# Gates behind the attention, recurrence and readouts ranked ahead, meta queries two blocks earlier, output projections in held order: a two-layer hybrid decoder trunk on one core

## The chip, the core and the metric

The kernel runs on one core of a Trainium2 chip. A core has TensorE (PE; its weight loads are listed as PEld), VectorE (DVE), ScalarE (ACT), GpSimd (POOL) and SyncE (SP), which here only issues DMAs. The metric is the device time of one execution in microseconds.

## The reference

The trunk has two layers of width 1024 over 16 learned meta tokens and 1024 tokens. One projection feeds two mixers: sliding-window attention with sinks (16 heads of 64, 2 key-value heads, meta tokens always visible) and an mLSTM matrix memory in chunkwise form (4 heads). Both are gated, concatenated and projected back.

```python
def hybrid_layer(x, ...):
    z = rms_norm(x, norm_g) @ w_in
    aq, ak, av, ag, mq, mk, mv, mi, mf, mo, mgate = split(z)
    q, k = rope(rms_norm(aq)), rope(rms_norm(ak))
    ya = sliding_window_sink_attention(q, k, av, sink) * silu(ag)
    mq, mk = split(silu(causal_conv(concat(mq, mk), conv_w, conv_b)))
    log_i, log_f = mi + b_i, log_sigmoid(mf + b_f)
    hm = rms_norm(mlstm_chunkwise(mq, mk, mv, log_i, log_f))
    ym = hm * sigmoid(mo) * silu(mgate)
    return x + concat(ya, ym) @ w_out
```

All of it is float32; the output is the 1024 token rows after the second layer.

## The kernel before

**Precision.** A float32 product is made of three fast ones: each operand is split into a rounded part (hi, an ACT copy) and the rest (lo, a subtraction on DVE or POOL), and hi*hi, hi*lo and lo*hi are summed in PSUM. So each weight tile and each activation needs a split before PE can use it. The tile `H` holds the normalised input of a layer, hi in rows 0 to 7 and lo in 8 to 15; in the output projection its 16 rows hold the hi parts of the 16 gated mixer outputs (`y`), and the units `ylo` hold their lo parts.

**Tiles.** The 1040 rows are cut into one tile of 16 (the meta tokens) and eight of 128 (`TT`), and for transposed results into three chunks of 272, 384 and 384 columns (`CH`).

**Memory that rotates.** `units` (16 large buffers), `t384` (5), `p512` (4), `w1k` (5), `raw` (2 buffers for weights as they land) and `RING` (8 split weight pairs) are pools: who takes a buffer waits until its last user is done. PSUM has eight banks: `pj` (2) for projections throughout, and either `S`, `T`, `O` for the attention or `pt`, `pss`, `po` (2 each) for the rest.

**Order.** A scheduler takes instructions in the order in which the program writes them, lets a ready one pass one that is not, and fixes an order for each engine before the run; each engine then works through its own queue in that order. `tc.high_priority(offset=EARLY)` ranks what stands in it 80 places ahead; `pin` keeps PE's instructions in the written order while `in_order` is set, which is the case from the first query projections to the end of the attention (L1000 on) and nowhere in the output projection.

**A layer.**
- `kv_tasks`: keys and values of all nine tiles, projected by `projN` from `H`.
- Attention: eight pairs of heads `j`, each of nine query blocks (eight in layer 1, where the meta block isn't needed). A block goes through `s1` (scores, mask, exponential, scale), `s2` (transposes of the probabilities and their split, L665 to L679), `s3` and `s4` (products with the values, readout at L707, gate), each some steps behind the other, woven with the query, gate and value projections of the next pairs (L222). In layer 0 the meta queries of pair j + 1 are transposed in `s3` of block 5 of pair j, in the bank of its result, and split into their unit by `q_put` (L561 to L564) in `s4` of the same block. The first block of pair j + 1 then uses them.
- `gates`: the log gates and their running sums and maxima for the whole sequence (L732 to L775), a serial chain over ACT, DVE and PE, written after the attention.
- mLSTM: for each of the four heads nine chunks in three steps `sa`, `sb`, `sc_` (state update, numerator and denominator, transposed result), woven with the remaining projections: values (`v_tasks`), convolution (`conv_tasks`) and output gates (`mo_tasks`). Their PSUM results are read out by an ACT instruction each (L793, L819, L838, L841).
- Output projection: all 16 `y` are loaded from DRAM (`spool`) and split first (L1100 to L1109, 48 splits in all), then four groups follow: the tiles up to 4 with the left and the right half of the columns, then tiles 5 to 8 with the left and the right half. A group runs 16 weight tiles (`wout`: load L172, hi on ACT L174, lo L175 on DVE for every third, else on POOL) against its tiles, 3 products of 512 columns each (L1135). The last group keeps its last 8 weights and finishes tile by tile. For a finished tile the residual is loaded (L1154), added (L1157) and stored; in layer 0 the sum of squares is taken (L1162) and, with the right half, `norm_tile` normalises the tile and transposes it into `H` (L277 to L292) for the next layer.

Of the kernel before, what the change touches and what calls it, by code (L numbers as in the profile page):

```python
# [62 lines left out]
def build(ctx, tc, I, O):  # L63
# [103 lines left out]

    def wout(l, k, c0, i):
# [3 lines left out]
        sy.dma_start(raw, I["w_out"][l][k * 128:(k + 1) * 128, c0:c0 + 512])  # L172
        hi, lo = [pair[:, a].rearrange("p a b -> p (a b)")[:, 0:512] for a in range(2)]
        sc.activation(hi, raw, AF.Copy)  # L174
        (ve if i % 3 == 2 else gp).tensor_tensor(lo, raw, hi, op=ALU.subtract)  # L175
# [98 lines left out]
    def norm_tile(t, xh, ssq_ap, gbc):  # L274
# [5 lines left out]
        for g in range(2):  # L280
            if gbc is None:
                ve.tensor_scalar(xh[g][:p, :], xh[g][:p, :], v[:p, 1:2], None, ALU.mult)
            for i in range(2 if gbc is not None else 0):
                xs = xh[g][:p, 256 * i:256 * i + 256]
                ve.scalar_tensor_tensor(xs, xs, v[:p, 1:2], gbc[2 * g + i][:p, 0:256], ALU.mult, ALU.mult)
            ps = bank("pt")
            for k in range(4):
                pin(pe.transpose(ps[:, k * p:(k + 1) * p], xh[g][:p, k * 128:(k + 1) * 128], ident[:p, :p]))
            src = ps[:, 0:4 * p].rearrange("p (k t) -> p k t", k=4)
            hi = H[:, 4 * g:4 * g + 4, t0:t0 + p]  # L290
            sc.activation(hi, src, AF.Copy)
            ve.tensor_tensor(H[:, 8 + 4 * g:12 + 4 * g, t0:t0 + p], src, hi, op=ALU.subtract)  # L292
            if t == 0:
                for i in range(3):
                    ve.tensor_copy(HM[:, 4 * g:4 * g + 4, 16 * i:16 * i + 16],
                                   H[:, 4 * (g + i // 2 * 2):4 * (g + i // 2 * 2) + 4, 0:16])
# [15 lines left out]
    def first_norm(t, xt, G):  # L312
# [9 lines left out]
        norm_tile(t, xg, st[:p, 0:2], None)  # L322
# [29 lines left out]

    for l in range(DEPTH):
# [11 lines left out]
        SS = []  # L365
        blk = [0, 0]
# [85 lines left out]
        def kv_tasks():  # L452
# [161 lines left out]
        def att_tasks(j, st):  # L614
# [67 lines left out]
            def s3(b):  # L682
# [12 lines left out]
            def s4(b):  # L695
# [10 lines left out]
                with tc.high_priority(offset=EARLY):  # L706
                    sc.activation(up[0:64, 0:2 * p], O[64:128, 0:2 * p], AF.Copy)  # L707
# [19 lines left out]
        def gates(GR):  # L727
# [4 lines left out]
            sc.activation(e, zf, AF.Abs)  # L732
# [54 lines left out]
        def v_tasks(h, wgf, st):  # L787
            def tile_task(t):
                p = TT[t][1]
                if t == 0:  # L790
                    v_units(st)
                ps = projN(wgf(), t, 256)
                sc.activation(st["V"](t)[:p, 0:256], ps[:p, 0:256], AF.Copy)  # L793
# [14 lines left out]
        def conv_tasks(h, wgf, st):  # L808
            def chunk_task(which, c):
# [9 lines left out]
                sc.activation(RAW[:, 3 + t0:3 + t0 + n], ps[:, :n], AF.Copy)  # L819
# [10 lines left out]
        def mo_tasks(u, wgf, st, held=None):  # L830
            def chunk_task(c):
# [6 lines left out]
                sc.activation(t1, ps[:, :n], AF.Tanh, scale=0.5)  # L838
                ps = projT(wgf(), 128, a, n)
                t2 = t384(n)  # L840
                sc.activation(t2, ps[:, :n], AF.Tanh, scale=0.5)  # L841
                ve.scalar_tensor_tensor(t2, t2, 1.0, ps[:, :n], ALU.add, ALU.mult)
# [11 lines left out]
        def m_tasks(h, st):  # L854
# [12 lines left out]
            def mm_split(out, a, b):  # L867
                for i, (x, y) in enumerate(((a[0], b[0]), (a[0], b[1]), (a[1], b[0]))):
                    pin(pe.matmul(out, x, y, start=(i == 0), stop=(i == 2)))

            def sa(c):
# [11 lines left out]
                if c < 8:  # L883
                    pk = bank("pt")
                    pin(pe.transpose(pk[:p, 0:128], kc, ident))
# [19 lines left out]
                pin(pe.matmul(pS[:p, :p], kc, qc, start=True, stop=True))  # L905
# [42 lines left out]
            def sc_(c):  # L948
# [5 lines left out]
                for f in range(2):  # L954
                    pin(pe.transpose(ph[:, 128 * f:128 * f + p], hs[:p, 128 * f:128 * f + 128], ident[:p, :p]))
# [4 lines left out]

            out = [begin]
            for c in range(11):
                if c < 9:
                    out.append(lambda c=c: sa(c))
                if 0 <= c - 1 < 9:
                    out.append(lambda c=c - 1: sb(c))
                if 0 <= c - 2 < 9:
                    out.append(lambda c=c - 2: sc_(c))
# [125 lines left out]
        for i, k in enumerate(order):  # L1094
# [92 lines left out]
```

## Time and profile before

| | us |
|---|---|
| median of 3 runs | 1997.38 |
| lowest and highest run | 1996.06, 1997.59 |
| the profiled execution | 1995.97 |
| its span (first to last instruction) | 1994.2 |

| busy in the span | PE | PEld | DVE | ACT | POOL |
|---|---|---|---|---|---|
| us | 1916.2 | 1806.1 | 1099.9 | 1062.6 | 929.9 |

The stages lie, by the timeline, at about 0 to 86 us (first norm, keys, first queries), 86 to 428 (attention), 428 to 828 (gates and mLSTM) and 828 to 1045 (output projection and norm) in layer 0, and up to 1394, 1800 and 1991 for the same ends in layer 1. A row of a window gives its length, each engine's busy time with the count of instructions, the granted share of PE's clock, the DMA share and GB/s. A row of a timeline gives start, length, engine, line, operation, output and inputs, count, and in brackets the idle time before it with what ended it. Matmuls overlap in PE, so one of 512 columns is listed with some 400 ns though one starts every 232 ns.

### The profile page before, as it was taken

What the parts mean: (1) busy time and instruction counts of PE and PEld (TensorE: products, weight loads), DVE (VectorE), ACT (ScalarE), POOL (GpSimd) and SP (SyncE); (2) the same over time, 40 slices, a digit from 0 to 9 for tenths busy, and PEclk for the clock granted to TensorE, in tenths of its full rate; (3) what the DMA queues carried; (4) which work ended last, traced back from release to release, by engine and by line L of the source; (5) the groups of instructions that cost most, each with busy time, mean ns of one, the idle gap of its engine ahead of it and who ended that gap; (6) DMA issues with size and microseconds to landing.
All of it is one profiled execution on the core that took longest, in us unless ns stands there. A gap on an engine that the chain in (4) does not pass through costs nothing. (4 is left out here: it accounts for less than half of the span.)

```text
span 1994.2 us, 36168 instructions
## 1 busy us (share of the span) xinstructions
PE 1916.2 (96%) x12823; PEld 1806.1 (91%) x12823; DVE 1099.9 (55%) x2969; ACT 1062.6 (53%) x3133; POOL 929.9 (47%) x1116
## 2 busy tenths in 40 slices
PE   6999899999999999989999999999999999999899
PEld 6899899999999999867879999999999999997787
DVE  8767767666445364541435677776573636347111
ACT  5567767655454544642324678777364545446221
POOL 7544544335555454553335345444365453646331
PEclk9999999999999999999999999999999999999999
DMA  5111111111212122453541111112122221217443
GB/s 160 43 33 42 42 44 37 35 53 45 57 47 69 36 59 58 146 170 115 162 144 49 48 36 51 45 36 58 38 58 62 39 76 38 61 47 232 145 141 106
DMA packets 149796, 147.71 MB, mean 74 GB/s; under 512 B 14952, under 2 KB 122768, under 8 KB 149616
## 3 DMA queue, kind: packets, MB, share of 16 engines
q1 hardware_dynamic: 149616, 145.41, 25.1%
q8 instruction: 101, 1.65, 0.4%
q14 instruction: 79, 0.65, 0.1%
HBM read 122.01 MB, written 23.29 MB: 73 GB/s over the span
## 5 line engine op out<-in xcount | busy, mean ns | idle before, releaser
L183 PE MATMUL pj<-H,RING 128*128 128x384 f32 (+2 forms) x3456 | 578.4, 323 | 0.3 <-ACT t L838 0.3
L183 PEld LDWEIGHTS pj<-H,RING 128*128 128x128 f32 x3456 | 546.1, 189 | 2.9 <-issue 0.7
L160 POOL TENSOR_TENSOR RING<-raw,RING 128x512 fp32r<-128x512 f32 (+1 forms) x196 | 260.6, 1337 | 137.8 <-ACT RING L159 125.4
L222 PE MATMUL pj<-RING,H 128*128 128x256 f32 (+1 forms) x1920 | 270.0, 287 | 1.9 <-DVE w1k L190 1.9
L222 PEld LDWEIGHTS pj<-RING,H 128*128 128x128 f32 x1920 | 244.0, 190 | 2.3 <-DVE w1k L190 2.2
L222 PE MATMUL pj<-H,RING 128*128 128x384 f32 (+2 forms) x1152 | 217.7, 327 | 3.0 <-DVE u L564 3.0
L175 POOL TENSOR_TENSOR RING<-raw,RING 128x512 fp32r<-128x512 f32 x88 | 115.0, 1311 | 196.8 <-ACT RING L174 192.4
L183 PE MATMUL pj<-RING,H 128*128 128x256 f32 x1536 | 200.8, 285 | 2.6 <-DVE H L292 1.5
L183 PEld LDWEIGHTS pj<-RING,H 128*128 128x128 f32 x1536 | 189.0, 189 | 4.0 <-DVE H L292 1.7
L174 ACT ACTIVATE RING<-raw 128x512 fp32r<-128x512 f32 x128 | 80.7, 632 | 202.2 <-DMA raw<-in_w_out_dram 134.1
L222 PEld LDWEIGHTS pj<-H,RING 128*128 128x128 f32 x1152 | 180.7, 191 | 3.8 <-PE T L668 1.3
L159 ACT ACTIVATE RING<-raw 128x512 fp32r<-128x512 f32 (+1 forms) x196 | 122.9, 629 | 73.3 <-DMA raw<-in_w_in_dram 48.2
L713 POOL TENSOR_TENSOR u<-u,w1k 128x128 f32<-128x128 f32 (+1 forms) x136 | 63.4, 466 | 176.8 <-DVE w1k L709 169.4
L175 DVE TENSOR_TENSOR RING<-raw,RING 128x512 fp32r<-128x512 f32 x40 | 31.5, 788 | 194.0 <-ACT RING L174 194.0
L679 POOL TENSOR_SCALAR_AFFINE_SELECT p<-p 128x512 fp32r<-128x512 f32 x112 | 72.2, 645 | 133.7 <-DVE p L675 131.1
L649 ACT ACTIVATE t<-S,mx 128x145 f32<-128x145 f32 (+1 forms) x272 | 100.3, 373 | 62.6 <-DVE mx L646 54.5
L882 POOL TENSOR_TENSOR p<-u,p 128x258 fp32r<-128x258 f32 x64 | 46.7, 730 | 169.2 <-ACT p L881 169.1
L1135 PE MATMUL pj<-RING,H 128*128 128x512 f32 x352 | 112.9, 400 | 7.1 <-DVE p L1157 5.8
L1135 PE MATMUL pss<-RING,H 128*128 128x512 f32 x352 | 113.5, 402 | 1.3 <-ACT H L1104 1.3
L824 DVE SCALAR_TENSOR_TENSOR t<-u,cw,t 128x384 f32<-128x384 f32 (+1 forms) x144 | 109.1, 757 | 2.6
L628 PE MATMUL S<-u 128*128 128x272 f32 (+2 forms) x544 | 87.5, 280 | 19.3 <-DVE u L563 16.3
L654 ACT ACTIVATE t<-t,mx 128x144 f32<-128x144 f32 (+1 forms) x272 | 97.6, 406 | 13.6 <-DVE mx L651 13.1
(342 smaller groups left out, 3834.0 us busy)
## 6 DMA issues: line engine op xcount, KB each, us to landing
raw<-in_w_out_dram SPq DMA_DIRECT2D x128, 256.0 KB, 2.8
raw<-in_w_in_dram SPq DMA_DIRECT2D x100, 256.0 KB, 2.8
raw<-in_w_in_dram SPq DMA_DIRECT2D x192, 128.0 KB, 2.3
spool<-u SPq DMA_DIRECT2D x56, 192.0 KB, 1.9
p<-x SPq DMA_DIRECT2D x24, 256.0 KB, 4.4
t<-spool SPq DMA_DIRECT2D x28, 192.0 KB, 3.5
p<-spool SPq DMA_DIRECT2D x28, 192.0 KB, 3.6
u<-em SPq DMA_DIRECT2D x8, 576.0 KB, 6.9
```

Of the source, the lines that this page charges most:

```text
L159: sc.activation(hi, raw[:, :, 0:o], AF.Copy)
L160: eng.tensor_tensor(lo, raw[:, :, 0:o], hi, op=ALU.subtract)
L174: sc.activation(hi, raw, AF.Copy)
L175: (ve if i % 3 == 2 else gp).tensor_tensor(lo, raw, hi, op=ALU.subtract)
L183: pin(pe.matmul(out, a, b, start=(i == 0), stop=(i == n - 1)))
L222: pin(pe.matmul(out(), x, y, start=(k + i == 0), stop=(k == n - 1 and i == 2)))
L628: pin(pe.matmul(S[:p, h, o + 2 - 2 * h:o + 2 - 2 * h + kn], lq, Ks[i][:, k0:k0 + kn], start=(i == 0), stop=(i == 1)))
L649: sc.activation(P[:p, 145 * h:145 * h + 145], S[:p, h, 1 + 127 * h:146 + 127 * h], AF.Exp, bias=mx[:p, 0, h:h + 1], accum_out=mx[:p, 1, h: ...
L654: sc.activation(Pn, Pn, AF.Copy, scale=mx[:p, 2, h:h + 1])
L679: gp.affine_select(OW, HL, [[0, 4], [1, 128]], ALU.is_ge, 0.0, base=0, channel_multiplier=-1)
L824: ve.scalar_tensor_tensor(z, RAW[:, t0 + i:t0 + i + n], wcol(i), z, ALU.mult, ALU.add)
L1135: pin(pe.matmul(ps[:p, :], a, b, start=(i + n == 0), stop=(i == 15 and n == len(terms) - 1)))
```

## The change

It has five parts. None adds or removes a product.

1. **Meta queries**: they are transposed and split in block 3 instead of block 5 of the pair before.
2. **Gates**: the first gate instruction on ACT is placed behind the attention's last readout (L707) by `tc.issue_after`.
3. **Ranks**: the readouts of the value, convolution and output-gate projections are ranked 80 places up. So are all steps of the recurrence (`ranked`), except its PE instructions (`there`), which keep their rank.
4. **Output projection**: the groups after the first keep the written order on PE. The splits of `y` are written between the weights: chunks 0 and 1 in the first group, chunk 2 in the second. Banks go in pairs. Three weights (six in the last group) are kept for the tile-by-tile end. Residual loads are issued behind the last weight load before them. The lo part of a weight goes to DVE for i = 9, 11, 13, 15 only.
5. **Norm between the layers**: `norm_tile` is cut into `norm_pre` (scale) and `norm_half` (four transposes and the split). Tiles 0 to 4 are reloaded and normalised during the third group, tiles 5 to 8 in the last; what is left over (`carry`) is run between the key projections of layer 1.

```diff
     def wout(l, k, c0, i):
-        sy.dma_start(raw, I["w_out"][l][k * 128:(k + 1) * 128, c0:c0 + 512])
+        w_load[0] = sy.dma_start(raw, I["w_out"][l][k * 128:(k + 1) * 128, c0:c0 + 512]).ins
...
-        (ve if i % 3 == 2 else gp).tensor_tensor(lo, raw, hi, op=ALU.subtract)
+        (ve if i > 8 and i % 2 else gp).tensor_tensor(lo, raw, hi, op=ALU.subtract)
...
                 ps = projN(wg, t, 256)
+                if l > 0 and t != 1 and carry:
+                    carry.pop(0)()
...
-                if b == 5 and j < 7 and first_q == 0:
+                if b == 3 and j < 7 and first_q == 0:
...
-                    sc.activation(up[0:64, 0:2 * p], O[64:128, 0:2 * p], AF.Copy)
+                    att_end[0] = sc.activation(up[0:64, 0:2 * p], O[64:128, 0:2 * p], AF.Copy).ins
...
-            sc.activation(e, zf, AF.Abs)
+            with tc.issue_after(att_end[0]):
+                sc.activation(e, zf, AF.Abs)
...
-                sc.activation(RAW[:, 3 + t0:3 + t0 + n], ps[:, :n], AF.Copy)
+                with tc.high_priority(offset=EARLY):
+                    sc.activation(RAW[:, 3 + t0:3 + t0 + n], ps[:, :n], AF.Copy)
...
+            def there(f, *a, **k):
+                with tc.high_priority(offset=-EARLY):
+                    pin(f(*a, **k))
...
-                    out.append(lambda c=c: sa(c))
+                    out.append(lambda c=c: ranked(sa, c))
...
-        pools = ["pj", "pss", "po"]
+        pools = ["pj", "pj", "pss", "pss", "po", "po"]
...
+            with tc.issue_after(w_load[0]):
+                sy.dma_start(xr[:p, :], src)
...
+        def norm_again(t):
+            t0, p = TT[t]
+            x = [p512(F32) for _ in range(2)]
+            for i in range(2):
+                sy.dma_start(x[i][:p, :], x1[t0:t0 + p, 512 * i:512 * i + 512])
+            norm_later(t, [y[:, o:o + 256] for y in x for o in (0, 256)])
...
+            in_order[0] = g > 0
...
+            cut = 10 if g == 3 else 13
+            chunks = ((0, 1), (2,), (), ())[g]
+            for i in range(cut):
+                for c in chunks:
+                    y_split(i, c)
+                w = wout(l, order[i], c0, i)
                 for t in grp:
+                    product(pss_t[t], i, t, w)
+                if g == 2 and not last:
+                    if i > 2:
+                        turn()
+                    if i % 2 and i < 10:
+                        norm_again(i // 2)
...
+            for t in grp:
+                for i, w in tail:
+                    product(pss_t[t], i, t, w)
+                    if g == 3 and i == 12:
+                        turn(3)
+                if g == 3:
+                    turn(2)
+                result(pss_t[t], t, hf)
+        in_order[0] = False
+        carry[:] = turns
```

`turn` runs the oldest waiting `norm_half` if enough of them wait; `norm_later` runs `norm_pre` and queues the two halves.

More of the change, by code (lines that the diff above doesn't have):

```diff
@@ L321, in first_norm @@
             xg.append(y)
-        norm_tile(t, xg, st[:p, 0:2], None)
+        norm_pre(t, xg, st[:p, 0:2], None)
+        for g in range(2):
+            norm_half(t, g, xg[g:g + 1])
     snk = cp.tile([128, 2, HEADS], F32, name="snk")
@@ L365, in build @@
         SS = []
+        att_end = [None]
         blk = [0, 0]
@@ L868, in mm_split @@
                 for i, (x, y) in enumerate(((a[0], b[0]), (a[0], b[1]), (a[1], b[0]))):
-                    pin(pe.matmul(out, x, y, start=(i == 0), stop=(i == 2)))
+                    there(pe.matmul, out, x, y, start=(i == 0), stop=(i == 2))
+            def there(f, *a, **k):
+                with tc.high_priority(offset=-EARLY):
+                    pin(f(*a, **k))
             def sa(c):
@@ L884, in sa @@
                     pk = bank("pt")
-                    pin(pe.transpose(pk[:p, 0:128], kc, ident))
+                    there(pe.transpose, pk[:p, 0:128], kc, ident)
                     kt = KQ[:p, 0:128], KQ[:p, 128:256]
@@ L959, in sc_, with ranked @@
                                   scale=cw[:, l, 40 + u:41 + u])
+            def ranked(f, c):
+                with tc.high_priority(offset=EARLY):
+                    f(c)
             out = [begin]
@@ new lines, in build, with product @@
+        pools = ["pj", "pj", "pss", "pss", "po", "po"]
+        nb = [0]
+        turns = []
+        def product(ps, i, t, w):
+            k = order[i]
+            t0, p = TT[t]
+            wh, wl = w
+            if t == 0:
+                st = ylo[k][:, L:L + 48]
+                terms = ((st, wh), (st, wl))
+                p = 48
+            else:
+                hi, lo = H[:, k, t0:t0 + p], ylo[k][:, t0:t0 + p]
+                terms = ((hi, wh), (hi, wl), (lo, wh))
+            for n, (a, b) in enumerate(terms):
+                pin(pe.matmul(ps[:p, :], a, b, start=(i + n == 0), stop=(i == 15 and n == len(terms) - 1)))
@@ new lines, in result @@
+        def result(ps, t, hf):
+            t0, p = TT[t]
+            c0 = 512 * hf
+            xr = p512(F32)
+            if l > 0:
+                src = x1[t0:t0 + p, c0:c0 + 512]
+            elif t == 0:
+                src = I["meta"][:, c0:c0 + 512]
+            else:
+                src = I["x"][t0 - 16:t0 + 112, c0:c0 + 512]
+            with tc.issue_after(w_load[0]):
+                sy.dma_start(xr[:p, :], src)
+            if t == 0:
+                ve.tensor_tensor(xr[:16, :], ps[32:48, :], xr[:16, :], op=ALU.add)
+            ve.tensor_tensor(xr[:p, :], ps[:p, :], xr[:p, :], op=ALU.add)
+            if last:
+                sy.dma_start(O["out"][t0 - 16:t0 + 112, c0:c0 + 512], xr[:p, :])
+                return
+            if hf == 1 and t > 4:
+                x0 = [t384(256) for _ in range(2)]
+                for i, x in enumerate(x0):
+                    sy.dma_start(x[:p, :], x1[t0:t0 + p, 256 * i:256 * i + 256])
+            sy.dma_start(x1[t0:t0 + p, c0:c0 + 512], xr[:p, :])
+            sc.activation(bank("pt")[:p, :], xr[:p, :], AF.Square, accum_out=ssq[:p, t, hf:hf + 1])
+            if hf == 1 and t > 4:
+                norm_later(t, x0 + [xr[:, 0:256], xr[:, 256:512]])
```

157 lines of the change are left out of this document (66 added, 91 removed).

## The prediction

> **What bounds the kernel now.** I read the page first, then a table of busy time by stage, then the list of TensorE's own waits, and then the timeline at the longest of them. The page says which engine carries the span:
>
> ```profile
> span 1994.2 us, 36168 instructions
> PE 1916.2 (96%) x12823; PEld 1806.1 (91%) x12823; DVE 1099.9 (55%) x2969; ACT 1062.6 (53%) x3133; POOL 929.9 (47%) x1116
> ```
>
> TensorE is busy for 96%, and the change adds and removes no matmul. So the change can win only what PE idles (1994.2 - 1916.2 = 78 us), and what PE loses to a lower clock after an idle stretch. By stage (columns: length, then busy PE, weight loads, VectorE, ScalarE, GpSimd, granted clock):
>
> ```profile
> 450.00:800.00 350.00, 347.73 (x2423) 341.75 (x2422) 175.32 (x515) 177.16 (x532) 183.52 (x236) 1.00 0.20 53
> 1450.00:1750.00 300.00, 300.00 (x2102) 297.31 (x2102) 152.59 (x431) 150.14 (x440) 158.90 (x198) 1.00 0.23 57
> ```
>
> The mLSTM stage, where the ranks change, is full (350 - 347.7 = 2.3 us idle in layer 0, none in layer 1): ranking can win nothing there. The idle time lies elsewhere, and PE's wait list names it (total us, times, longest):
>
> ```profile
> PE S L628 <- DVE u L563: 16.3, 8, 5.9
> ...
> PE T L665 <- DVE ptm L676: 6.3, 4, 2.8
> PE pj L1135 <- DVE p L1157: 5.8, 1, 5.8
> ...
> PE pj L1135 <- POOL RING L175: 2.3, 1, 2.3
> PE po L869 <- DVE w1k L933: 2.1, 2, 1.1
> ...
> PE po L1135 <- ACT RING L174: 1.8, 1, 1.8
> ...
> PE pj L1135 <- ACT H L1104: 1.3, 1, 1.3
> PE po L1135 <- POOL RING L175: 1.3, 2, 0.7
> PE pss L1135 <- ACT H L1104: 1.3, 1, 1.3
> ```
>
> Three parts of the change meet three of these groups: the meta queries (L563, 16.3), the end of the attention (L676, 6.3) and the output projection (L1135: 5.8 + 2.3 + 1.8 + 1.3 + 1.3 + 1.3 = 13.8). Short windows around the gaps show the clock, the figure after the busy times:
>
> ```profile
> 248.00:254.00 6.00, 5.65 (x37) 5.51 (x38) 3.29 (x12) 2.76 (x11) 4.27 (x4) 0.70 0.33 90
> 328.00:334.00 6.00, 4.18 (x23) 4.04 (x24) 3.51 (x12) 2.90 (x11) 5.04 (x4) 0.72 0.39 105
> 414.00:420.00 6.00, 4.71 (x20) 4.74 (x21) 4.46 (x11) 2.48 (x5) 2.42 (x5) 0.72 0.24 63
> ...
> 894.00:900.00 6.00, 6.00 (x22) 4.73 (x22) 0.78 (x3) 2.18 (x7) 1.28 (x1) 0.77 0.83 253
> ...
> 1394.00:1400.00 6.00, 6.00 (x29) 6.00 (x28) 3.01 (x8) 2.25 (x4) 1.47 (x4) 0.72 0.17 44
> ...
> 1856.00:1863.00 7.00, 5.44 (x13) 4.37 (x14) 3.08 (x5) 1.86 (x4) 2.55 (x2) 0.52 0.65 210
> ```
>
> A busy stretch of 6 us at 0.72 loses 0.28 x 6 = 1.7 us. So a removed gap also returns about 1.7 us of clock.
>
> **The change part by part.**
>
> *Meta queries two blocks up.* In layer 0 each pair's first block (16 queries) waits for the split of its meta queries, which is now transposed in block 3 instead of 5, so some two blocks earlier:
>
> ```profile
> L628 PE MATMUL S<-u 128*16 128x16 f32 x32 | 3.1, 174 | 16.0 <-DVE u L563 15.4
> ```
> ```profile
> 241.45 0.92 PE L222 MATMUL pj<-H,RING 128*128 128x272 f32 x6
> 248.27 0.50 PE L628 MATMUL S<-u 128*16 128x16 f32 x4 [5.90 <-DVE u L563]
> ```
> ```profile
> 244.94 0.71 ACT L654 ACTIVATE t<-t,mx 128x144 f32<-128x144 f32 x2
> ```
>
> The whole wait is 15.4 us. What is late next is the softmax scale of the block before (L654), without which PE's next transposes (L665) can't run. In the longest case 13 matmuls stand before them, no more than 2 us by the row of 6 in 0.92: PE would come to them between 244.0 and 244.4. But the scale ends at 244.94 + 0.71 = 245.65: I let 1.7 us stay. For the six short gaps together I take 1.2 us that stay (an estimate: most are no longer than the work that stands between). Gain 15.4 - 2.9 = 12.5 us; bounds 7 and 15.4. Of the clock I count the loss at 328 alone, 1.7 us; the one at 248 may stay with its remainder. **14.2 us.** The instructions that move (a 16-column transpose, two small ACT copies, two small DVE subtractions) are the same and move on PE, ACT and DVE alone; their unit of memory is taken two blocks earlier, when the first half of the old queries has just been read for the last time.
>
> *Gates behind the attention.* The gates' Abs, Exp and Ln stand in ScalarE's queue ahead of the attention's last copies, with a table load:
>
> ```profile
> 410.95 1.28 ACT L734 ACT_TABLE_LOAD   x1
> ...
> 427.76 0.38 ACT L707 ACTIVATE w1k<-O 64x256 f32<-64x256 f32 x1 [0.83 <-PE O L704]
> ```
> ```profile
> 415.29 0.27 PE L665 MATMUL T<-cst,t 128*32 128x128 f32 x1 [2.85 <-DVE ptm L676]
> ...
> 432.21 0.27 PE L737 MATMUL po<-cst,GT 128*36 128x128 f32 x1
> ```
> ```profile
> 1393.77 0.27 PE L665 MATMUL T<-cst,t 128*32 128x128 f32 x1 [2.43 <-DVE ptm L676]
> ```
>
> The copies L672 and L673 come late by it, and PE's next transposes wait 2.85 us here and 2.43 in layer 1: 5.3 us. I leave 0.5 in each for the copy's own chain: 4.3, and 2 x 1.7 of clock (rows 414 and 1394). **7.7 us.** The added wait: the Abs now stands behind the last L707, which ends at 428.1. With the 1.28 load and some 0.9 of small work the gates end near 430.4, before PE takes their transposes at 432.2; so it costs nothing, and behind the waiting Abs stand the convolution's copies, which two banks of projection cover. If that cover fails, the recurrence begins up to 2 us later in each layer: bounds of this cost -4 to +5.3.
>
> *Readouts and recurrence 80 places up.* They reorder ACT, DVE and POOL in a stage in which PE is full, while the recurrence's matmuls keep their rank. Value 0; from the trace at most the 2.3 us idle above to win, and on the other side the third rival.
>
> *Output projection.* The splits of the gated outputs spread (32 in the first group, 16 in the second, instead of all 48 ahead); the groups after the first keep the written order on PE; banks rotate in pairs; VectorE takes no weight split before the tenth. The longest gap shows what this meets:
>
> ```profile
> 1856.21 0.69 DVE L175 TENSOR_TENSOR RING<-raw,RING 128x512 fp32r<-128x512 f32 x1 [8.16 <-ACT RING L174]
> 1856.82 0.68 DVE L1157 TENSOR_TENSOR p<-pj,p 128x512 f32<-128x512 f32 x1
> ```
>
> VectorE stood 8.16 us at a weight split whose load was late, the finished bank's sum (L1157) behind it, and PE waited 5.8 us for the bank. With weights on GpSimd and fresh banks for the new group this gap has no cause left. Of the 13.8 us I keep both starts of the first group (L1104, 2.6): gain 11.2. Clock: 0.23 x 6 = 1.4 at 894 and 0.48 x 5.44 = 2.6 at 1856. **15.2 us.** GpSimd gets one split more in sixteen, hidden in its 53% of idle time; were it not, that is the first rival. The residual loads stand behind the group's last weight load on SP and before its results; their cover is the tail of three weights, and the next weights stand behind them on SP.
>
> *Norm of layer 1 in held order.* Its half tiles' transposes are now fixed places on PE: five tiles are reloaded whole (5 loads of 256 KB more), three halves are carried into the next projection. The chain behind a tile's last product:
>
> ```profile
> 1026.58 0.68 DVE L1157 TENSOR_TENSOR p<-pj,p 128x512 f32<-128x512 f32 x1
> ...
> 1031.20 1.29 DVE L292 TENSOR_TENSOR H<-pt,H 128x512 fp32r<-128x512 f32 x2 [0.47 <-ACT H L291]
> ...
> 1040.10 0.69 DVE L1157 TENSOR_TENSOR p<-po,p 128x512 f32<-128x512 f32 x1
> ...
> 1046.34 1.27 DVE L292 TENSOR_TENSOR H<-pt,H 128x512 fp32r<-128x512 f32 x2
> ```
>
> It takes 4.6 us quiet (1026.6 to 1031.2) and 6.2 beside GpSimd. The products of one tile's tail took, by the chain of waits:
>
> ```profile
> 1985.02 5.57 PE pj L1135 x24
> ```
>
> 5.57 / 24 = 0.232 us each. The tile in between now holds PE for 18 of them, 4.2 us, where it held it for 24. So 0.4 to 2.0 us can show at each of three tiles: 1.2 to 6; I take **3 us lost**.
>
> **Sum.** 14.2 + 7.7 + 0 + 15.2 - 3 = 34.1. The profiled execution took 1995.97 us (1.8 of it outside the span): 1961.9. The median is 1.4 above that execution: **1963 us**.
>
> *A rule against the clock term.* The Trainium skill, page "TensorE: Matmul & The Clock Gate", Part 1, says that the clock halves only after an idle window of about 3.4 us. By that rule only the gaps of 5.9 and 5.85 us cost clock, 5 us less would be won, and the sum would give 1968. The trace disagrees with it at 414, where the clock fell after 2.85 us of idle time.
>
> **The rivals.**
>
> *1. Weights starve the held order (slower).* PE in written order stops at any late weight, and a weight passes two raw buffers. How often weights came while splits were loaded too, and afterwards (ScalarE, 1802 to 1841 and 862 to 901):
>
> ```profile
> L174 ACT ACTIVATE RING<-raw 128x512 fp32r<-128x512 f32 x9 | 5.7, 630 | 7.1 <-DMA raw<-in_w_out_dram 6.2 <-PE pj L1135 0.8
> ```
> ```profile
> L174 ACT ACTIVATE RING<-raw 128x512 fp32r<-128x512 f32 x12 | 7.6, 632 | 23.2 <-DMA raw<-in_w_out_dram 23.2
> ```
>
> That is one in 39 / 9 = 4.3 us beside splits. PE uses one in 12 x 0.232 = 2.8 us in layer 1 and 14 x 0.232 = 3.25 in layer 0. If 4.3 stays in both groups with splits, beyond the eight held ahead, it costs 24 x 1.5 + 24 x 1.05 = 61 us: 2024. It eats the whole gain from a weight in 3.7 us on. Against it: that stretch carried 43 splits, and the new first group carries 32 in a longer time.
>
> *2. The projection's gaps only change their cause.* Weights at about 3 us, a bit over PE's pace, bring back the 15.2: 1978.5. For it: the second row, 3.25 us a weight, with 23.2 us of waiting for loads.
>
> *3. Ranks hold up the queues (no change).* A ranked instruction that waits for an unranked matmul keeps all behind it waiting:
>
> ```profile
> DVE w1k L906 <- PE pss L905: 90.5, 43, 3.6
> ```
> ```profile
> 812.57 4.37 PE L183 MATMUL pj<-H,RING 128*128 128x384 f32 x24
> ```
>
> These waits (2.1 us on average) are hidden while they stay under the 4.4 us that the other bank of projection lasts. If over some 70 chunks they outgrow it by 0.5 us each, 35 us go: 1997. The Trainium skill, "PSUM — Partial Sum Buffer", section "Engine vs sequencer instructions", says "ScalarE/VectorE/GpSimdE queues are strict FIFO", by which nothing could pass the waiting one; the trace agrees where L1157 stood behind L175 above.
>
> *4. Every named gap goes.* 15.4 + 5.3 + 13.8, the 2.1 of the recurrence's last chunks (L869, L933), and 1.8 + 1.7 + 1.7 + 1.7 + 1.4 + 2.6 = 10.9 of clock: 47.5, so 1950.
>
> **How the numbers follow.** Forecast 0.55 (1954 to 1974, by the bounds of its terms: 15.4 - 12.5 and 5.3 - 4.3 and 3 - 1.2 and 2.6 below, 12.5 - 7 and 6 - 3 and a gap or two above); second rival 0.18; fourth 0.12; first 0.09; third 0.06. Faster by over 0.2% (about what a measurement here can tell from no change): 0.55 + 0.18 + 0.12 = 0.85; within it 0.06; slower 0.09. The range runs from 1946 to 1989: at the lower end the fourth rival with the 2.3 us of the mLSTM stage and a clock drop more, at the upper end the second rival with the recurrence late by 4 us and the norm at its 6. The first and third rivals, 15%, are left out.
>
> **What would show it.** Right: the first block's S matmuls in layer 0 with under 4 us of waiting in all; no table load ahead of the attention's last L672; no gap over 2 us between the projection's groups; the recurrence stage as full as before. Wrong: L1135 waiting often for RING (first or second rival); L183 waiting for a pj readout (third); gaps at the norm's transposes over 6 us.

## The result and the profile after

The changed kernel took 1963.99 us (median of 4 runs, 1963.52 to 1965.07) against 1997.49 for the kernel before (4 runs, 1996.06 to 1998.13). The ratio is 0.9834, with a 95% interval from 0.9817 to 0.9851: 33.5 us faster. The prediction was 1963. It is the case held likeliest that came true, but three of its five terms were off, and their errors cancelled, as the experiments show.

The profiled execution took 1965.07 us, 30.9 less than that of before. The page of the changed kernel:

```profile
span 1963.3 us, 36174 instructions
...
PE 1904.4 (97%) x12823; PEld 1794.8 (91%) x12823; DVE 1090.0 (56%) x2961; ACT 1070.1 (55%) x3133; POOL 938.8 (48%) x1124
```

PE's idle time fell from 78.0 to 1963.3 - 1904.4 = 58.9 us, so 19.1 of the 30.9 were idle time. The other 11.8 are PE's busy time, 1916.2 before and 1904.4 now, for the same 12823 matmuls. That is the clock: behind the first 40 us the trace of before has twelve steps of 3.41 us at half clock, with PE busy for 33.9 us of them, and the trace of after has two, with 6.5 us. Half of the difference, 13.7 us, is an estimate of what came back, and covers the 11.8. The prediction had 25 and 9.1.

The mLSTM stages and the two output projections as windows (columns as before):

```profile
440.00:790.00 350.00, 350.00 (x2442) 344.14 (x2441) 173.63 (x519) 182.36 (x538) 182.38 (x237) 1.00 0.20 54
1420.00:1720.00 300.00, 300.00 (x2111) 297.44 (x2111) 151.72 (x445) 154.04 (x448) 157.31 (x201) 1.00 0.22 55
...
817.10:1022.30 205.20, 204.73 (x920) 161.83 (x921) 82.45 (x149) 79.17 (x179) 92.55 (x94) 0.99 0.54 171
1777.30:1959.60 182.30, 180.99 (x778) 144.78 (x778) 51.45 (x80) 57.37 (x111) 73.66 (x61) 1.00 0.52 165
```

And the two projections in the kernel before:

```profile
830.10:1039.30 209.20, 203.56 (x897) 159.16 (x898) 79.89 (x148) 78.12 (x177) 84.86 (x90) 0.98 0.50 159
1801.20:1990.60 189.40, 183.48 (x775) 147.79 (x775) 53.61 (x76) 55.93 (x111) 71.66 (x58) 0.97 0.50 156
```

The recurrence stage is as full as before, or fuller. In the projections PE idled 5.64 and 5.92 us and idles 0.47 and 1.31 now. Layer 0's projection does more than before in less time: 23 matmuls more lie in it (920 for 897), transposes of the norm.

The list of PE's waits after the change (total us, times, longest). Lines have moved: L628 is now L640, L665 is L677, L676 is L688, L692 is L704, L709 is L721, L222 is L224, L563 and L564 are L575 and L576, L1104 is L1133, L1135 is L1159, and L174 and L175 are L176 and L177.

```profile
PE O L704 <- DVE w1k L721: 5.5, 8, 1.7
...
PE O L704 <- DVE u L576: 2.6, 4, 1.1
...
PE pss L1159 <- ACT H L1133: 2.1, 1, 2.1
...
PE pj L1159 <- ACT H L1133: 1.9, 1, 1.9
...
PE po L1159 <- POOL RING L177: 0.9, 1, 0.9
```

The 16.3 us of the first block (S for u L563) have all but gone: one wait of 0.9 us is left. So have the waits of the projection for a bank and for RING, but for 0.9. The start of the projection waits more than before (2.1 and 1.9 for H, 1.3 and 1.3 before). New at the top are waits of the attention: O products for a readout (w1k, 1.8 us in four times before) and O products for the meta queries' own split (u L576, none before). That is where part of the first term went.

### The profile page after: what moved, and what is told of

Read it like the earlier page. It is cut to its first block, busy times and chain, and to the rows that moved or that the text cites. A ratio compares the mean times of both kernels' runs of the same rounds, so it can differ in the third digit from the quotient of the medians.

```text
span 1963.3 us, 36174 instructions
## 1 busy us (share of the span) xinstructions
PE 1904.4 (97%) x12823; PEld 1794.8 (91%) x12823; DVE 1090.0 (56%) x2961; ACT 1070.1 (55%) x3133; POOL 938.8 (48%) x1124
## 4 chain that ended last, share of the span: by engine, by line
PE 78%; DVE 7%; ACT 5%; issue 3%; DMA 3%; POOL 3%; SPq 0%; ACTq 0%; POOLq 0%; DVEq 0%
PE pj L185 34%; PE pj L224 13%; PE pss L1159 7%; PE pj L1159 6%; PE po L1159 4%; PE po L890 2%; PE S L640 2%; PE pss L890 2%; PE O L716 2%; PE O L704 1%; DMA raw<-in_w_in_dram 1%; PE pt L890 1%; POOL RING L160 1%; DMA raw<-in_w_out_dram 1%; ACT t L661 1%
## 5 line engine op out<-in xcount | busy, mean ns | idle before, releaser
L224 PE MATMUL pj<-RING,H 128*128 128x256 f32 (+1 forms) x1920 | 269.8, 287 | 4.1 <-DVE u L613 2.2
L224 PEld LDWEIGHTS pj<-RING,H 128*128 128x128 f32 x1920 | 243.9, 190 | 4.8 <-DVE u L613 2.4
L224 PE MATMUL pj<-H,RING 128*128 128x384 f32 (+2 forms) x1152 | 215.4, 325 | 4.3 <-DVE u L576 4.3
L185 PE MATMUL pj<-RING,H 128*128 128x256 f32 x1536 | 206.9, 285 | 3.4 <-DVE H L298 1.4
L177 POOL TENSOR_TENSOR RING<-raw,RING 128x512 fp32r<-128x512 f32 x96 | 125.6, 1314 | 174.8 <-ACT RING L176 166.7
L224 PEld LDWEIGHTS pj<-H,RING 128*128 128x128 f32 x1152 | 178.6, 188 | 5.2 <-issue 2.8
L176 ACT ACTIVATE RING<-raw 128x512 fp32r<-128x512 f32 x128 | 80.8, 632 | 174.8 <-DMA raw<-in_w_out_dram 155.8
L1159 PE MATMUL pss<-RING,H 128*128 128x512 f32 x384 | 120.6, 396 | 2.1 <-ACT H L1133 2.1
L1159 PE MATMUL pj<-RING,H 128*128 128x512 f32 x352 | 110.1, 395 | 1.9 <-ACT H L1133 1.9
L859 DVE SCALAR_TENSOR_TENSOR t<-t,pj 128x384 f32<-128x384 f32 (+2 forms) x48 | 24.5, 511 | 128.1 <-ACT t L858 128.1
L721 DVE TENSOR_TENSOR w1k<-O,w1k 64x128 f32<-64x128 f32 (+1 forms) x272 | 74.6, 274 | 37.4 <-ACT w1k L719 34.8
```

The lines of the kernel that those rows point to most:

```text
L177: (ve if i > 8 and i % 2 else gp).tensor_tensor(lo, raw, hi, op=ALU.subtract)
L185: pin(pe.matmul(out, a, b, start=(i == 0), stop=(i == n - 1)))
L224: pin(pe.matmul(out(), x, y, start=(k + i == 0), stop=(k == n - 1 and i == 2)))
L721: ve.tensor_tensor(y[64 * h:64 * h + 64, :p], O[0:64, p * h:p * h + p], up[0:64, p * h:p * h + p], op=ALU.add)
L1159: pin(pe.matmul(ps[:p, :], a, b, start=(i + n == 0), stop=(i == 15 and n == len(terms) - 1)))
```

## The experiments

Times are medians; where two kernels of different sets are compared, it is by their ratios to the kernel before, which ran beside each.

### The parts, one at a time, on the kernel before

**Meta queries alone.**

```diff
-                if b == 5 and j < 7 and first_q == 0:
+                if b == 3 and j < 7 and first_q == 0:
```

> The kernel before with the meta queries alone moved from block 5 to block 3. Theory of the prediction (the wait at the first block goes and little takes its place): 12 to 14 us faster, about 1983.5. Rival drawn from the trace after (the split now stands in block 3's own bank, and the products of the blocks behind it wait for the readout and the split; of the 15.4 us only some 6 are won as idle time, and 3.4 us of clock come back): 7 to 10 us faster, about 1988.5. The first-block waits at the S matmuls go in both; they differ in whether waits at the O products grow by 5 us or more.

Measured: 1990.26 us against 1996.8, ratio 0.9968 (0.9956 to 0.998), 6.4 us faster. Its waits of PE, and one row of the kernel before:

```profile
PE O L692 <- DVE w1k L709: 7.1, 8, 1.7
...
PE O L692 <- DVE u L564: 2.6, 4, 1.1
```
```profile
PE O L692 <- DVE w1k L709: 1.8, 4, 0.8
```

The first-block waits are gone, and the O products wait 7.1 + 2.6 where they waited 1.8: 7.9 us more. Of the 21.5 us that PE idled in the attention of layer 0 (342.00 - 320.48 in the windows below) only 3.4 are saved; the rest of the gain in this stage is the clock (0.98 to 1.00):

```profile
85.70:427.70 342.00, 320.48 (x2422) 311.65 (x2421) 238.32 (x717) 239.92 (x805) 147.29 (x202) 0.98 0.15 41
```
```profile
83.90:418.60 334.70, 316.56 (x2422) 307.39 (x2420) 239.87 (x718) 239.21 (x806) 146.65 (x202) 1.00 0.15 42
```

The first window is the kernel before, the second this one. The rival holds in its mechanism: the waits of the O products grew by more than its 5 us. The gain lies just under its 7 to 10 us, and its idle part is 3.4 us, not some 6. One step of the clock that came back here, at the end of the attention, is owed to where a gap fell and not to the edit (last section).

**Gates alone.**

```diff
-            sc.activation(e, zf, AF.Abs)
+            with tc.issue_after(att_end[0]):
+                sc.activation(e, zf, AF.Abs)
```

> The kernel before with the gates alone placed behind the attention's last readout. Theory of the prediction: both gaps before the last transposes (2.85 and 2.43 us) go but for 0.5 each, and two spells of low clock with them: 7.7 us faster, about 1990. Rival drawn from the trace after (0.94 and 1.68 us of the two gaps stay): 2.7 us of idle time and 3.4 of clock, 6 us faster, about 1991.5. A third one: the gates are late and the recurrence starts later, so that under 3 us are won; then the first recurrence matmuls wait by 1 us or more beyond what they wait before.

Measured: 1989.13 us, ratio 0.9963 (0.9952 to 0.9975), 7.4 us faster: both of the first two are inside the interval, the third is out. The time can't tell the first two apart. The trace can: 0.95 and 1.70 us of the two gaps stay, as the second had it.

**Ranks alone** (the readouts and the recurrence 80 places up, as in the change, and nothing else).

> The kernel before with the ranks alone (readouts and recurrence 80 places up, the recurrence's matmuls kept). Theory of the prediction: the stage is full, so nothing changes, 0 with at most 2.3 us won. Rival drawn from the trace after: the mLSTM stages together took 4.7 us less, and if the ranks did that, this kernel is 4 to 6 us faster (about 1992.5) and the gain lies at the first chunks and at the last ones. The prediction's third rival (the ranked instructions hold up their queues): 5 us or more slower, with projections waiting for readouts.

Measured: 1994.09 us, ratio 0.999 (0.9977 to 1.0003): 2.0 us faster, with an interval from 0.6 slower to 4.6 faster. So the third rival of the prediction is out, and whether the ranks win a little isn't settled. They also cost something at the end of the recurrence of layer 0, where the last chunk's product waits for a readout (1.08 us in the kernel before). PE's timeline with ranks alone:

```profile
827.27 0.60 PE L877 MATMUL po<-p,w1k 128*128 128x258 f32 x3 [3.01 <-DVE w1k L941]
```

**Output projection and norm alone** (everything of parts 4 and 5).

> The kernel before with the new output projection and norm alone (spread splits, held order, banks in pairs, weight splits off VectorE, halves of the norm). Theory of the prediction: 15.2 us won in the projections and 3 lost at the norm, 12.2 faster, about 1985.5. Reading of the trace after: 4.0 and 7.1 us won in the projections and 3.75 us won, not lost, between the layers: 15 us faster, about 1982.5. The sum of the four kernels tells whether the parts add: if they do, their gains make 33.5 us together; if one part does what another does too, the sum is larger than that.

Measured: 1977.1 us, ratio 0.9898 (0.988 to 0.9916): 20.4 us faster, the largest part by far, and more than either expectation. The four gains make 6.4 + 7.4 + 2.0 + 20.4 = 36.2 against 33.2 for the whole (0.0166 x 1997.5); within these intervals the parts add.

### The whole, with one part taken back

**Without the ranks.**

> The changed kernel without the ranks (readouts and recurrence as before, the rest as changed). If the ranks are worth nothing (theory of the prediction, and an interval of the ranks alone that holds 0): within 3 us of the changed kernel's 1964, 1961 to 1967. If they are worth their part by themselves even beside the other parts: 1967 to 1969, and the waits at the first recurrence matmuls (0.7, 1.2 and 2.0 us before) come back. If their cost at the recurrence's end (first product of the projection 2.12 and 1.90 us late in the changed kernel, 1.1 without ranks) outweighs it: 1960 to 1962.

Measured: 1967.04 us, ratio 0.9848 (0.9829 to 0.9867), beside 0.9834 (0.9817 to 0.9851) for the whole: 2.8 us slower, with intervals that overlap. Together with the ranks alone it points to 2 or 3 us in their favour, and doesn't settle it.

**Without the held order in the projection.**

```diff
-            in_order[0] = g > 0
+            in_order[0] = False
```

> The changed kernel with no written order on PE in the output projection (the scheduler's own order in all four groups and the norm; all else as changed). If the held order is what closed the projection's gaps and the one at the norm: the gaps come back, 8 us or more slower, about 1973. If the fresh banks, the weight splits off VectorE and the spread splits of y closed them: within 3 us of 1964. The prediction's first rival (held order makes PE wait for weights) would show as a gain, 1961 or less.

Measured: 1968.51 us, ratio 0.9857 (0.984 to 0.9875), 4.6 us slower; the intervals just overlap. The windows say where (layer 0's projection, the way to the next attention, layer 1's projection; this kernel first, then the changed kernel's second window):

```profile
818.90:1020.60 201.70, 201.31 (x892) 158.45 (x893) 79.24 (x146) 78.16 (x177) 92.34 (x94) 0.99 0.55 174
1020.60:1078.80 58.20, 54.01 (x444) 53.61 (x443) 34.77 (x70) 24.96 (x53) 26.39 (x23) 0.97 0.19 51
1782.80:1963.30 180.50, 180.06 (x778) 144.93 (x778) 48.79 (x79) 57.44 (x111) 73.56 (x61) 1.00 0.52 166
```
```profile
1022.30:1073.90 51.60, 49.86 (x416) 48.78 (x415) 32.97 (x68) 23.32 (x51) 26.36 (x23) 1.00 0.22 57
```

The gaps inside the projections do **not** come back: PE idles 0.39 and 0.44 us, and in layer 1, where there is no norm, this kernel's projection is 1.8 us shorter. The loss is all between the layers, where the norm's transposes come late and PE stands 4.19 us:

```profile
1031.24 4.53 PE L185 MATMUL pj<-RING,H 128*128 128x256 f32 x24 [4.19 <-ACT u L501]
```

So in these traces the held order is a cure for the norm and not for the projection. To hold it in layer 0 alone was not tried.

**VectorE takes every third weight again.**

```diff
-        (ve if i > 8 and i % 2 else gp).tensor_tensor(lo, raw, hi, op=ALU.subtract)
+        (ve if i % 3 == 2 else gp).tensor_tensor(lo, raw, hi, op=ALU.subtract)
```

> The changed kernel with every third weight split on VectorE again in the output projection (as before; four of sixteen late ones in the changed kernel). If a late weight on VectorE with a finished bank's sum behind it was what made the 5.85 us gap and still can: a gap of over 2 us between groups again, 3 to 8 us slower. If the new rotation of the banks suffices: within 2 us of 1964.

Measured: 1966.63 us, ratio 0.9848 (0.9831 to 0.9866), 2.8 us slower with overlapping intervals, and no gap between groups: in its projections PE idles 0.2 and 0.0 us. Then the new banks might suffice; so both were taken back together:

```diff
-        pools = ["pj", "pj", "pss", "pss", "po", "po"]
+        pools = ["pj", "pss", "po"]
-        (ve if i > 8 and i % 2 else gp).tensor_tensor(lo, raw, hi, op=ALU.subtract)
+        (ve if i % 3 == 2 else gp).tensor_tensor(lo, raw, hi, op=ALU.subtract)
```

> The changed kernel with both the old rotation of banks (one of each pool in turn) and every third weight split on VectorE. Each of the two alone may be enough of a cure for the 5.85 us gap (with the weights on VectorE and the new rotation the projections idled 0.2 and 0.0 us). If so, this one shows a gap of 3 us or more between groups again and is 5 to 10 us slower than the changed kernel's 1964, about 1971. If neither matters and the spread splits did it: within 2.5 us of 1964.

Measured: 1965.05 us, ratio 0.984 (0.9824 to 0.9857), the same as the whole change, and its projections are full:

```profile
818.10:1022.20 204.10, 204.10 (x918) 161.64 (x918) 78.90 (x148) 77.75 (x176) 86.89 (x91) 0.99 0.53 169
1779.00:1958.20 179.20, 179.16 (x777) 144.65 (x775) 52.62 (x79) 55.33 (x109) 69.12 (x58) 1.00 0.52 165
```

Neither the banks nor the engine of the weight splits was needed for the 5.85 us gap to go. Left are the spread of the splits, the shorter tail and the place of the residual loads. (The change also writes the squares of a finished tile in layer 0 to a `pt` bank instead of the tile's own; no run takes that by itself, and it can't bear on the gap of layer 1, where no squares are taken.)

**All splits of y ahead of the first group again.**

```diff
+        for i in range(16):
+            for c in range(3):
+                y_split(i, c)
...
-            chunks = ((0, 1), (2,), (), ())[g]
+            chunks = ()
```

> The changed kernel with all 48 splits of the gated outputs written ahead of the first group again, as before, and nothing else undone. If late weights behind those splits made the gaps of the first groups (2.25 us at 865, 0.6 to 1.8 us at 888 to 893 before): some 5 us of waits for RING come back in layer 0 and with a held order they cost more than before, 1969 or above, and the prediction's first rival (held order starved of weights) is seen where it would have struck. If the banks were the cure for these too: within 2.5 us of 1964.

Measured: 1982.14 us, ratio 0.9931 (0.9915 to 0.9946): 19.4 us slower than the change. PE's waits and one of them in layer 0, then how often weights came on ScalarE in the first 39 us of layer 1's projection; last the same row of the changed kernel:

```profile
PE pj L1159 <- ACT RING L176: 9.7, 2, 5.7
...
845.92 0.63 PE L1159 MATMUL pj<-RING,u 128*48 128x512 f32 x1 [4.05 <-ACT RING L176]
...
L176 ACT ACTIVATE RING<-raw 128x512 fp32r<-128x512 f32 x5 | 3.2, 631 | 8.2 <-DMA raw<-in_w_out_dram 8.1
```
```profile
L176 ACT ACTIVATE RING<-raw 128x512 fp32r<-128x512 f32 x9 | 5.7, 629 | 4.5 <-DMA raw<-in_w_out_dram 4.5
```

Five weights came in 39 us with the splits ahead; nine, one in 4.3, with the splits spread. The five are no steady stream: SyncE issued no weight load from 1781 to 1808, only loads of y, and PE stood when the eight weights held ahead were used up. So weights do starve PE here, for 13.0 us in all (9.7 for the hi parts, 3.3 for the lo parts). But it is not the held order of the prediction's first rival that they starve: all four waits stand in the first group (817 and 1785 on), whose order isn't held (`in_order` is set for g > 0). Nor do splits ahead alone do it: in the kernel before, which has them ahead too, nine weights came in these 39 us (the first rival's row). What else kept the weights back here was not taken apart, so the 19.4 us are no measure of the spread; the next run is.

**The spread alone, on the kernel before** (the splits written as in the change; order, banks, engines, tail and residual loads as before).

```diff
+                chunks = () if grp[-1] == 8 else ((0, 1), (2,))[hf]
...
                 for i, k in enumerate(order[:cut]):
+                    for c in chunks:
+                        y_split(i, c)
                     w = wout(l, k, c0, i)
```

> The kernel before with the spread of the splits of y alone (chunks 0 and 1 written between the weights of the first group, chunk 2 between those of the second), with PE's order, the banks, VectorE's weights, the last group's eight held weights and the residual loads as before. The whole new projection and norm won 20 us (1977.1 against 1996.8); the held order is worth some 4 of them beside the rest, new banks with VectorE's weights nothing. If the spread is the cure by itself: 12 to 16 us faster, 1981 to 1985, and the 5.85 us gap of layer 1 is gone as well. If it cures the first groups alone and that gap (VectorE at a late weight, a finished bank's sum behind it) needs one of the other parts: the gap stays, with its 3.4 us of clock, and this one is 5 to 9 us faster, 1988 to 1992.

Measured: 1980.27 us, ratio 0.9916 (0.9901 to 0.993): 16.8 us faster. It is by itself the cure, and the long gap is gone too. PE's windows of the projections and its place at the change of groups:

```profile
827.70:1029.10 201.40, 201.40 (x897) 159.46 (x898) 78.29 (x148) 78.37 (x177) 85.52 (x90) 0.99 0.52 165
1789.60:1971.50 181.90, 181.02 (x775) 145.87 (x775) 54.69 (x76) 56.42 (x110) 71.13 (x58) 0.99 0.52 164
...
1840.84 0.73 PE L1139 MATMUL pj<-RING,H 128*128 128x512 f32 x2 [0.88 <-DVE p L1163]
```

The wait for the finished bank's sum is still there, at 0.88 us for 5.85. The weight at which VectorE stood, ahead of that sum, tells why; ScalarE's timeline in this kernel, then in the kernel before:

```profile
1838.83 0.63 ACT L174 ACTIVATE RING<-raw 128x512 fp32r<-128x512 f32 x1 [2.58 <-DMA raw<-in_w_out_dram]
```
```profile
1855.55 0.63 ACT L174 ACTIVATE RING<-raw 128x512 fp32r<-128x512 f32 x1 [3.59 <-DMA raw<-in_w_out_dram]
```

Counted from the projection's first product (1789.6 and 1801.2) it came at 49.2 us instead of 54.4, while PE reached the bank at 50.4 (1840.84 less 0.88, less 1789.6) and 50.5 (1857.56 less 5.85, less 1801.2). So the weight was 5 us late with the splits ahead, and PE met that at the first place where a bank hung on it. The lag opens between the groups: the first group's last weight came at 34.8 us in this kernel and at 35.0 in the kernel before. SyncE's queue in the kernel before shows what stood there:

```profile
1837.96 0.33 SPq L172 DMA_DIRECT2D raw<-in_w_out_dram  x1
1839.39 1.75 SPq L1154 DMA_DIRECT2D p<-x  x4
1841.22 16.04 SPq L172 DMA_DIRECT2D raw<-in_w_out_dram  x7
```

The four residual loads were issued when a split of y on VectorE (L1109) had ended at 1839.4, and the next weights stood behind them. With the splits spread they had all gone out by 1817.9, before the group's last weights. This is read from the queue; no run moves the residual loads alone.

### Another place for the meta queries

The attention has one bank O, and the change lets the transposed meta queries sit in it while two copies and two subtractions run. Two experiments put them into spare columns of a score bank instead (S has two). In the first, the transpose stood behind block 6's exponentials:

```diff
-                if b == 3 and j < 7 and first_q == 0:
-                    st["QM"] = O[:, 256:272]
-                    q_meta_turn(j + 1, st["QM"])
...
                 live[b] = P
+                if b == 6 and j < 7 and first_q == 0:
+                    with tc.high_priority(offset=EARLY):
+                        q_meta(j + 1, S[:, 0, 300:316])
```

> The changed kernel with the transposed meta queries in spare columns of a score bank (S, two of them, transposed and split behind the scores of block 6, about the same moment) and no longer in the one bank of the results (O). If that single bank, held some microsecond longer by the two copies and two subtractions, is why the move won 6.5 us and not 14: the waits of O products for the meta queries' split go, 2.6 us and what follows from them, 3 to 5 us faster, 1959 to 1961. If the rest is the attention's own chain over ScalarE and VectorE, which only shows itself once the long wait is gone: within 1.5 us of 1964.

Measured: 1987.02 us, ratio 0.9946 (0.9928 to 0.9964), 22 us slower than the change. The transpose (L595) writes other columns than the exponentials read, and still waited for them. PE's waits:

```profile
PE S L595 <- ACT t L661: 17.1, 7, 3.7
```

So it tested something else than it was meant to. In the second the transpose stands right behind the score matmuls, ahead of the exponentials, and the copies follow them:

```diff
+                meta = b == 6 and j < 7 and first_q == 0
+                if meta:
+                    q_meta_turn(j + 1, S[:, 0, 300:316])
                 if st.setdefault("S", 0) < 2:
...
                 live[b] = P
+                if meta:
+                    q_put(q_unit(j + 1, 0)[:, 1024:1056], S[:, 0, 300:316], 16)
```

> The changed kernel with the meta queries transposed into a score bank right behind the scores of block 6, ahead of the exponentials in the program (the run before had the transpose behind them, and PE waited 17.1 us for their ends: S L595 <- ACT t L661). Theory that the one bank of the results held back the gain of the move: those 17.1 us go, and so do the 2.6 us of waits of O products for the split; 3 to 5 us faster than the changed kernel, 1959 to 1961. Theory that the attention's own chain over ScalarE and VectorE bounds it: within 1.5 us of 1964, with the waits of O products for readouts (w1k, 5.5 us) as large as before or larger.

Measured: 1963.0 us, ratio 0.9832 (0.9815 to 0.9848): no difference from the change that can be measured. PE's waits and its window of layer 0's attention, then that window of the changed kernel:

```profile
PE O L706 <- DVE w1k L723: 3.0, 4, 1.5
...
83.90:414.60 330.70, 317.97 (x2422) 309.43 (x2421) 235.19 (x716) 236.15 (x800) 147.70 (x202) 0.99 0.15 42
```
```profile
85.20:417.50 332.30, 316.62 (x2422) 307.43 (x2420) 239.27 (x717) 236.83 (x800) 147.39 (x202) 1.00 0.15 42
```

The waits of O for the split go, and those for readouts fall from 5.5 to 3.0; PE idles 12.7 us in the stage instead of 15.7. Of these 3 us a clock drop at 243 took 1.7 back in this execution, and the total shows nothing. So the bank held back some 3 us of idle time. By the time the second theory holds, but the waits for readouts fell, which it didn't expect. That what else of the 15.4 didn't come is the attention's own chain over ScalarE and VectorE is read from the waits that are left (readouts 3.0 here); no run changed that chain.

No version beat the change by more than its measurement can tell.

## Why the prediction was right, and where it wasn't

**Meta queries: 14.2 predicted, 6.4 (4.0 to 8.8) measured alone.** The mechanism holds, the wait went. The step that failed is "What is late next is the softmax scale of the block before (L654)", and with it the 1.7 us that were let stay. In the longest case of the changed kernel PE's timeline shows:

```profile
243.58 0.27 PE L677 MATMUL T<-cst,t 128*32 128x128 f32 x1 [0.88 <-DVE ptm L688]
...
245.76 0.48 PE L704 MATMUL O<-p,u 128*128 128x256 f32 x2 [1.69 <-DVE w1k L721]
```

and ScalarE's:

```profile
242.88 0.57 ACT L545 ACTIVATE u<-pj 128x512 f32<-128x512 f32 x1
243.36 0.57 ACT L546 ACTIVATE pj<-pj 128x512 f32<-128x512 f32 x1
243.95 0.38 ACT L719 ACTIVATE w1k<-O 64x256 f32<-64x256 f32 x1
```

Late next was the readout of O: L719 stood behind 1.1 us of the next queries' copies in ScalarE's queue, then the sum on VectorE that PE waited for (L721, from 245.05) behind 0.7 us of a reduction of the same queries (L549). There is one bank O, so PE had to wait. 0.88 + 1.69 = 2.6 us stay here. In the short cases new waits of about 1 us each took the place of waits of 0.9 to 2.4. The prediction followed what the meta queries need and left out what they occupy: it named their unit of memory and not their bank. By the second run with another place for them, the bank is some 3 us of the 9 that lack in idle time (12.5 predicted, 3.4 seen); the rest is put down to the chain of readouts, which was not tested.

**Gates: 7.7 predicted, 7.4 (5.0 to 9.6) measured alone.** Right in mechanism. The size agrees within the interval, but its idle part was off: not 0.5 but 0.94 and 1.68 us of the two gaps stay, so 2.7 us of idle time are won, not 4.3. With the 3.4 of clock that makes 6.1, which the interval holds as well as 7.7. The cover held; ScalarE's timeline of the changed kernel has the load right behind the last readout:

```profile
417.50 0.38 ACT L719 ACTIVATE w1k<-O 64x256 f32<-64x256 f32 x1 [0.83 <-PE O L716]
...
418.29 1.28 ACT L747 ACT_TABLE_LOAD   x1
```

**Ranks: 0 predicted with at most 2.3 to win, 2.0 (-0.6 to 4.6) measured alone.** Nothing in the runs contradicts it.

**Output projection and norm: 15.2 - 3 predicted, 20.4 (16.8 to 24.0) measured alone.** Three things in it.

First, the cause. "With weights on GpSimd and fresh banks for the new group this gap has no cause left" names two edits that beside the spread are worth nothing that could be measured; the spread does the work (16.8 of the 20.4 alone, with intervals that overlap). The late weight had been read rightly; that the splits ahead had made it late was not.

Second, the clock term, 1.4 + 2.6, was sized by windows of 6 us. At 890 and at 1856 the clock was halved for two steps of 3.41 us each, and for one more at 1801, which the prediction left out. PE was busy for 5.07, 5.17 and 3.41 us of them, and half of that, 6.8 us, was lost. After the change one step is left, at 818, with PE busy for 3.10 us. So 5.3 us came back, not 4.

Third, the norm. The 3 us of loss were a sum of uncovered chains; the products of the next tile cover them (0.47 us idle in the whole window). The prediction took no account of a gap that stood in the kernel before; PE's timeline there, and after the change at the same place:

```profile
1047.07 1.97 PE L288 MATMUL pt<-cst,p 128*128 128x128 f32 x8 [2.00 <-DVE H L292]
```
```profile
1022.98 0.44 PE L294 MATMUL pt<-cst,t 128*128 128x128 f32 x2 [0.27 <-DVE t L286]
...
1025.78 0.66 PE L294 MATMUL pt<-cst,p 128*128 128x128 f32 x4 [0.24 <-ACT pt L1185]
1026.98 3.11 PE L185 MATMUL pj<-RING,H 128*128 128x256 f32 x24 [0.55 <-ACT u L501]
...
1031.21 0.66 PE L294 MATMUL pt<-cst,p 128*128 128x128 f32 x4 [0.68 <-DVE H L298]
```

The four short waits make 1.7 us for the 2.0, and the half-clock step behind the old gap is gone: some 2 us won, none lost.

**The first rival** didn't come, and its sum was wrong. One weight in 4.3 us is the changed kernel's own rate in layer 1's first group, and PE doesn't starve there. The rival counted the eight weights held ahead as eight fewer late ones (24 x 1.5 + 24 x 1.05 = 61), but they are also time in hand: the last of 32 weights comes after 24 x 4.3 = 103 us, and PE asks for it after 31 x 2.8 = 87 in layer 1 and 31 x 3.25 = 101 in layer 0. That is some 19 us, 1982 and not 2024. The run with all splits ahead also measured 1982, but by chance: its waits came in the group that isn't held, from a stretch without any weight.

So the sum came out right by luck: an excess of 8 us in the first term met a lack of 8 in the last two.

## What to carry to other kernels

When a wait is to go by starting something earlier, follow what the earlier start occupies as well as what it needs: a bank that exists once is a queue. When transfers that are needed at once and transfers that are needed later share a path, write the later ones between the first; it was worth more here than order, banks and engines together. And count the clock with the idle time: of the 30.9 us that the profiled execution lost, 11.8 were PE's own pace.

## What the runs showed of the hardware

PE's clock is not set by the length of a gap but by a fixed grid. In all 14 traces every half-clock stretch that lies wholly inside the span lasts 3.41 us or a multiple of it, and within a trace their starts lie on one grid of 3.41 us (in the kernel before 57.1, 244.8, 330.1 and 415.5: 55, 25 and 25 steps apart). The page "TensorE: Matmul & The Clock Gate" of the Trainium skill, Part 1, states a free-running window of 3413 ns; the traces agree. What decides is how much of one window PE idles. The end of the attention in three steps of this grid (length, then PE's busy time; the clock behind the other engines), in the kernel before:

```profile
412.10:415.50 3.40, 0.55 (x5) 0.38 (x5) 2.18 (x5) 2.08 (x7) 1.94 (x3) 1.00 0.31 80
415.50:418.90 3.40, 3.40 (x13) 3.40 (x12) 2.80 (x8) 2.24 (x4) 1.48 (x4) 0.50 0.28 74
```

and with the meta queries alone, where the same gap (2.85 us before, 2.77 here) falls across two windows:

```profile
403.10:406.50 3.40, 1.80 (x16) 1.57 (x14) 0.86 (x2) 3.32 (x9) 2.33 (x2) 1.00 0.38 111
406.50:409.90 3.40, 2.23 (x14) 2.26 (x15) 3.25 (x9) 1.75 (x4) 1.87 (x4) 1.00 0.39 101
409.90:413.30 3.40, 3.40 (x24) 3.40 (x23) 1.48 (x3) 1.50 (x5) 0.46 (x3) 1.00 0.00 0
```

2.85 us of idle time in one window halve the next; 1.60 and 1.17 in two windows cost nothing. Over the 14 traces, behind the first 40 us: of 60 windows in which PE idled over 1.95 us, 60 were followed by half clock; of 195 with 0.9 to 1.55 us, four; between 1.55 and 1.95 us, 16 of 48. The limit lies at about half a window, 1.7 us. The four are windows that ran at half clock themselves, and for those the limit is lower: 15 idled 0.92 us or more, and each was followed by another; of the 65 that idled 0.61 us or less, none. So by these counts a gap under some 1.5 us costs only itself if it is alone in its window, one over some 3.5 (twice the limit) always costs a step more, and between them it depends on where it falls: the same kernel can get or miss 1.7 us at each such gap. That may be why 29 runs of the kernel before spread from 1990.95 to 2003.02 us. Their granted clocks go with it: the six at 0.991 took 1990.95 to 1995.57 us, the five at 0.986 or 0.987 took 1999.43 to 2003.02. That it is the place of the gaps which moves the clock from run to run was not tested. The same page of the Trainium skill has a rule that the clock falls after an idle window of about 3.4 us, against which the prediction set a gap of 2.85: the traces show that half of the window is enough. By that rule the terms at 328, 414, 894 and 1394 would have gone, 6.5 us of the prediction's clock and not its 5.
